# Second-layer modulation parts moved from TensorE to GpSimd, during the first layer's feed-forward

## The chip, the core and the metric

The kernel runs on one core of one Trainium2 chip. The metric is the device time of one execution in microseconds (us). Five engines with queues of their own work side by side: TensorE (PE, with its weight loads as PEld), VectorE (DVE), ScalarE (ACT), GpSimd (POOL) and SyncE (SP). Each takes its instructions in the order in which the build put them. A DMA is issued from the queue of an engine, here SP or POOL, and runs on 16 DMA engines that all share.

## What is computed

A backbone of two layers over 256 latent tokens and 256 context tokens, 1024 channels wide. Each layer forms six modulation vectors from a conditioning vector, and uses them as shift, scale and gate:

```python
mod_l = (silu(c) @ w_mod[i] + b_mod[i])          # latents;  w_mod[i] is 1024 x 6144
mod_c = (silu(c_ctx) @ w_mod[i] + b_mod[i])      # context
sh1, sc1, g1, sh2, sc2, g2 = split(mod, 6)       # each 1024 wide
u   = modulate(rmsnorm(x, norm1_w[i]), sh1, sc1) @ w_in[i]
x   = x + g1 * branch_merge(ssd(u), attention(u), gates(u))
h   = modulate(rmsnorm(x, norm2_w[i]), sh2, sc2)
x   = x + g2 * conv_ffn(h)
```

The last layer (i = 1) gives its result for the latents alone: the context tokens take part only through the first part (sh1, sc1) of its modulation. Its parts g1, sh2, sc2 and g2 are read for latents alone.

## The kernel before

**Tiles and products.** Channels lie on the 128 partitions and tokens along a row, 512 tokens in layer 0 and 256 or 512 in layer 1. Each weight tile is 128 x 1024 numbers (four blocks of 128 rows by 256 columns, 512 KB). It is loaded by SP into `raw`, split by ACT into a rounded part `whi` and by DVE into the rest `wlo` (`split_w`, L313 and L314), and each product takes three matmuls: `whi` with the high part of the activations (`th`), `whi` with the low part (`tl`), `wlo` with `th`. `gemm_f` (L393 to L395 and L407 to L409), `gemm_halves` (L425 to L427, where the two halves s = 0 and s = 1 of 256 tokens are finished one after the other) and `gemm_t` (L441 to L443) do this. They get their tiles from `take`.

**Work in the gaps.** Generators stand in lists. `lanes` hold attention heads, scan steps and norms, and advance by a step every few matmuls. `trickle` holds the modulation parts: `take` advances it by one step for each weight tile. One part g covers 2048 of the 6144 columns of `w_mod[i]`, so a layer has g = 0 (sh1, sc1), g = 1 (g1, sh2) and g = 2 (sc2, g2). `mod_part` works a part off in 16 steps. A step loads 512 KB of `w_mod` on SP's queue into `mraw` (two buffers), and multiplies it with four fp32 matmuls of 32 columns of weights (`s2`, the vectors silu(c) and silu(c_ctx) among zeros) by 256 columns (L465). In the profile one such matmul is two records. At the end the bank goes through ACT and eight records of transposes (L472) to the columns `mod`. Parts (0,1), (0,2) and (1,0) run during layer 0's mixer, parts (1,1) and (1,2) during layer 1's mixer.

**Norms.** `Stats.rstd` sums squares with two matmuls (`pystat`, L516), and DVE makes `ms` of them. POOL raises `ms` to the power of -1/2 (`rs`, L521), DVE writes a diagonal `dg`, and TensorE spreads it (L493). Then for each of the eight blocks of 128 channels `mod_block` runs DVE (`lnv`, L541), ACT twice (`th` L542 and `lnv` L546) and POOL (`tl`, L547). The norm ahead of layer 0's feed-forward is called once for each half, s = 0 and s = 1, from L1098. The norm at the head of layer 1 is queued from L1151 during the last products of the feed-forward. POOL has little else to do: the subtractions of the scan (L969) and its products (L925), and some small DMAs.

**The feed-forward of layer 0.** `w_up` takes 44 weight tiles and `w_down` 30. The last two products of `w_down` have 256 columns each (s = 0 and s = 1), the others 512 after the first two.

**What sets the order.** The order in which instructions stand on each engine is set when the program is built. It follows the code, except that an instruction may be moved ahead of others where the builder holds its inputs to be ready. Buffers of one tag are reused in turn, and the next writer waits for the last reader.

Of the kernel before, what the change touches and what calls it, by code (L numbers as in the profile page):

```python
# [10 lines left out]
F32 = mybir.dt.float32  # L11
F32R = mybir.dt.float32r
AF = mybir.ActivationFunctionType
ALU = mybir.AluOpType
AX = mybir.AxisListType

P = 128
D = 1024
KD = D // P
# [40 lines left out]
def hybrid_backbone_kernel(  # L60
# [7 lines left out]
    V, A, G, T = nc.vector, nc.scalar, nc.gpsimd, nc.tensor  # L68

    base = ctx.enter_context(tc.tile_pool(name="base", bufs=1))  # L70
    wp = ctx.enter_context(tc.tile_pool(name="wp", bufs=1))
    lp = ctx.enter_context(tc.tile_pool(name="lp", bufs=1))
# [3 lines left out]
    def nm(s):  # L76
        cnt[0] += 1
        return f"{s}_{cnt[0]}"

    def bank(tag, what=""):  # L80
        return psp.tile([P, 512], F32, tag=tag, name=nm("p" + tag + what), bufs={"mm": 2, "s": 3, "y": 2, "m": 1}[tag])
# [11 lines left out]
    ident = kt[:, C_ID:C_ID + P]  # L93
# [5 lines left out]
    sinT = kt[:, C_SIN:C_SIN + SEQ]  # L99
    mhalf = base.tile([P, 4], F32, name="mhalf")  # L100
    V.memset(mhalf, -0.5)


    dp = ctx.enter_context(tc.tile_pool(name="dp", bufs=1, space=bass.MemoryType.DRAM))
# [24 lines left out]
    col = []  # L129
# [85 lines left out]
    def boot_load(f):  # L215

        raws = []
        for v in range(2):
            for kq in range(2):
                raw = bp.tile([P, 4, 256], F32, tag="boot", name=nm("boot"), bufs=8)  # L220
                nc.sync.dma_start(raw, kview(w_mod[0], 1024 * (1 - v) + 256 * f, 256, 4 * kq, 4))
                raws.append((raw, v, kq))
        return raws

    def boot_mod(raws):
        ps = bank("s", "mod")
        for raw, v, kq in raws:
            for j in range(4):
                T.matmul(ps[32 * j:32 * j + 32, v * 256:v * 256 + 256], s2[:, 4 * kq + j, :], raw[:, j, :],
                         start=kq == 0 and v == 0, stop=kq == 1 and v == 1)  # L230
        row = lp.tile([P, 512], F32, tag="g", name=nm("modrow"), bufs=4)
        A.copy(row, ps)
        return row
# [19 lines left out]
    with tc.tile_pool(name="rows", bufs=2) as rp:  # L253
# [4 lines left out]
        raws = boot_load(0)  # L258
# [7 lines left out]
        ps = bank("s")  # L266
        T.transpose(ps[:, 0:16], r0, ident[0:16, 0:16])
        s2 = base.tile([P, KD, 32], F32, name="s2")
# [7 lines left out]
        row = boot_mod(raws)  # L276
        load_cols(0, rows0)
        boot_cols(0, row)
        for s in range(2):
# [6 lines left out]
            for j in range(0, KD, 2):  # L286
                ps = bank("s")
# [33 lines left out]
    def fill(n, pinned=False):  # L321
        load(n)
        while loaded and len(ready) < n:
            ready.append(split_w(*loaded.pop(0), pinned))
# [2 lines left out]
    lead = [1]  # L327
    lanes = ([], [])
    trickle = []

    def advance(queue):

        while queue:
            try:
                return next(queue[0]) is not None
            except StopIteration:
                queue.pop(0)
        return False
# [6 lines left out]
    def drip():  # L345
        advance(trickle)
# [9 lines left out]
    def flush():  # L356
        while trickle:
            drip()

    def take(n_tiles):  # L360
        ws = []
        for _ in range(n_tiles):
            fill(1)
            ws.append(ready.pop(0))
            load(DL)
        for _ in range(n_tiles):
            drip()
        fill(lead[0])
        return ws
# [87 lines left out]
    def mod_part(i, g, pool, ps):  # L457

        for half in range(2):
            for k in range(KD):  # L460
                raw = pool.tile([P, 4, 256], F32, tag="mraw", name=nm("mraw"), bufs=2)
                src = w_mod[i, k * P:(k + 1) * P, g * 2048:(g + 1) * 2048]
                nc.sync.dma_start(raw, src.rearrange("p (j h n) -> p h j n", j=4, h=2)[:, half])
                for j in range(4):
                    T.matmul(ps[32 * j:32 * j + 32, half * 256:half * 256 + 256], s2[:, k, :], raw[:, j, :],  # L465
                             start=k == 0, stop=k == KD - 1)
                yield 1
        row = lp.tile([P, 512], F32, tag="g", name=nm("modrow"), bufs=4)
        A.copy(row, ps)
        pt = bank("s")  # L470
        for b in range(4):
            T.transpose(pt[:, b * P:(b + 1) * P], row[:, b * P:(b + 1) * P], ident)  # L472
        m = col[i]["mod"]
        for v in range(2):
            V.tensor_tensor(
                m[:, g * 16:(g + 1) * 16, v].rearrange("p (j b) -> p b j", j=4),
                pt.rearrange("p (b j r) -> p b j r", b=4, j=4)[:, :, :, v],
                col[i]["bm"][:, g * 16:(g + 1) * 16].rearrange("p (j b) -> p b j", j=4), op=ALU.add)
        if g == 0:
            a, sc, nw = col[i]["a1"], m[:, 8:16, :], col[i]["n1"]  # L480
        elif g == 2:
            a, sc, nw = col[i]["a2"], m[:, 32:40, :], col[i]["n2"]
        else:
            return
        V.scalar_tensor_tensor(a, sc, 1.0, nw.unsqueeze(2).to_broadcast([P, KD, 2]), op0=ALU.add, op1=ALU.mult)


    def spread(pool, rs, s, ps):
# [86 lines left out]
    for i in range(DEPTH):  # L575
        if i:
            L = col[i]
            m = L["mod"]
        full = i < DEPTH - 1
# [37 lines left out]
        if i == 0:  # L617
# [3 lines left out]
            L = col[0]  # L621
            m = L["mod"]
            for f in range(4):
                whi, wlo, _ = split_w(*load_w(plan.pop(0)))
                if f < 3:
                    raws = boot_load(f + 1)
# [7 lines left out]
                for cc in range(2):  # L634
                    for fb in range(2):
                        cs = slice(fb * P, fb * P + P)
                        for kk in range(2):
                            k = 2 * f + kk
# [4 lines left out]
                    if cc == 0 and f < 3:  # L643
                        row = boot_mod(raws)
# [2 lines left out]
        xd = park_x(i, N)  # L647
        mst = ExitStack()
        mp = mst.enter_context(tc.tile_pool(name=f"mp{i}", bufs=1))
        mb = bank("m", "mod")  # L650
        trickle.extend(mod_part(*lg, mp, mb) for lg in (((0, 1), (0, 2), (1, 0)) if full else ((1, 1), (1, 2))))
        mg = [mp.tile([P, N], F32, name=f"mg{i}_{j}") for j in range(KD)]
        BF = [mp.tile([P, 512], F32, name=f"BF{i}_{j}") for j in range(4)]
        CF = [mp.tile([P, N], F32, name=f"CF{i}_{j}") for j in range(4)]
# [118 lines left out]
        for z in kLz:  # L773
            for cc in range(2):
                q = slice(64 - 64 * cc, 128 - 64 * cc)
# [38 lines left out]
        ps = bank("mm", "dt")  # L814
        for n, x in enumerate((hh, hl)):
            for k in range(KD):
                T.matmul(ps[32 * (k % 4):32 * (k % 4) + 32, :], wdt[:, k, :], x[k].bitcast(F32),
                         start=n == 0 and k < 4, stop=n == 1 and k > 3)
        if True:
            raw = lp.tile([P, 512], F32, tag="g", name=nm("dtr"), bufs=4)  # L820
            A.copy(raw, ps)
            pt = bank("s")
# [35 lines left out]
            for t in range(4):  # L858
                for dr in range(2):
                    r = 32 * t + 16 * dr  # L860
# [173 lines left out]
        for p in range(4):  # L1034
            for f, o in enumerate(gemm_f(hh, hl, N, KD)):
                j = 2 * p + f
# [26 lines left out]
        for p in range(4):  # L1063
            for f, o in enumerate(gemm_f(yh, yl, N, KD)):
                j = 2 * p + f
# [38 lines left out]
        fp = fst.enter_context(tc.tile_pool(name=f"ff{i}", bufs=1))  # L1104
        fh = [fp.tile([P, N], F32R, name=f"fh{i}_{k}") for k in range(KF)]
        fl = [fp.tile([P, N], F32R, name=f"fl{i}_{k}") for k in range(KF)]
        def ff_conv(ps, n, dst, r):
            conv3(ps, n, dst, lambda k: L["fw"](k, r), L["fb"](r))

# [26 lines left out]
        if full:  # L1136
            st = Stats(lp)
            for p in range(3):
                for f, o in enumerate(gemm_f(fh, fl, N, KF)):
                    for s in range(2):  # L1140
                        residual(2 * p + f, o[:, 256 * s:256 * s + 256], 40, s)
                        st.add(xF[2 * p + f][:, 256 * s:256 * s + 256], s)
            flush()
            hh, hl = operand(lp)
            for s in range(2):
                for f, o in enumerate(gemm_f(fh, fl, 256, KF, 256 * s)):
                    if f == 0:
                        drain()
                    residual(6 + f, o, 40, s)
                    st.add(xF[6 + f][:, 256 * s:256 * s + 256], s)  # L1150
                lanes[0].append(ln_steps(st, lp, i + 1, col[i + 1]["a1"], 0, s, hh, hl))  # L1151
        else:

            st = Stats(lp)
            fwb = fp.tile([P, D], F32, name="fwb")
            G.dma_start(fwb, final_norm_w.partition_broadcast(P))
            ot = [fp.tile([P, D], F32, name=f"ot{t}") for t in range(2)]
            for p in range(4):
                pt = bank("s")
                for f, o in enumerate(gemm_f(fh, fl, N, KF)):  # L1160
                    j = 2 * p + f
                    residual(j, o, 40, 0)
                    st.add(xF[j][:, 0:256], 0)
                    for t in range(2):
                        T.transpose(pt[:, t * 256 + f * P:t * 256 + (f + 1) * P], xF[j][:, t * P:(t + 1) * P], ident)
                for t in range(2):
                    A.copy(ot[t][:, 256 * p:256 * p + 256], pt[:, t * 256:(t + 1) * 256])
            rs, _ = st.rstd(0, D)
            for t in range(2):
                for e in range(2):  # L1170
                    es = slice(512 * e, 512 * e + 512)
                    V.scalar_tensor_tensor(ot[t][:, es], ot[t][:, es], rs[:, t:t + 1], fwb[:, es], op0=ALU.mult, op1=ALU.mult)
                    (nc.sync if e else nc.scalar).dma_start(out[0, t * P:(t + 1) * P, es], ot[t][:, es])
        flush()
        fst.close()


# [29 lines left out]
```

## Time and profile before

| | |
|---|---|
| time, median of 3 runs | 1745.26 us (1743.87 to 1746.32) |
| the profiled execution | 1740.01 us, its span 1738.2 us |
| granted clock of TensorE, mean | 0.993 |
| instructions | 27022 |
| PE busy | 1667.1 us, 96% |
| DVE busy | 1148.0 us, 66% |
| ACT busy | 848.2 us, 49% |
| POOL busy | 181.3 us, 10% |
| DMA | 240.71 MB, 138 GB/s in the mean |

The busy times are sums over stages with different limits. In the profile's rows a line of an engine gives count, busy time and mean duration of a group. In answers by time the columns are start, duration, engine, line, operation, what is written and read, the form, the count, and in brackets the idle time before it with what ended it. Layer 0's mixer takes the time up to about 658 us, its output projection and second norm that up to about 715 us, its feed-forward that up to about 1081 us. Layer 1 follows.

### The profile page before, as it was taken

Reading aid. Unit: us, or ns where it says so; the run is one execution under the profiler, and the core shown is the slowest. Engines: PE = TensorE matmul, PEld = TensorE weight load, DVE = VectorE, ACT = ScalarE, POOL = GpSimd, SP = SyncE. Lnnn points to the kernel's source line nnn. Section 1 sums busy time; section 2 is a strip of 40 time slices with the busy share of each in tenths; the row PEclk is TensorE's granted clock in tenths of the full one; section 3 lists DMA queues with packets and bytes.
Section 4 is the critical chain, followed back from the end, with each engine's and each line's share of the span. In section 5 each row is a group of like instructions: output and inputs, shape, how many; then the busy total and the mean of one; then the engine's idle time right before and its main releaser. Section 6 shows DMA issues by size and latency. Waiting matters only on the chain. (4 is left out here: it accounts for less than half of the span.)

```text
span 1738.2 us, 27022 instructions
## 1 busy us (share of the span) xinstructions
PE 1667.1 (96%) x10547; PEld 1406.2 (81%) x10547; DVE 1148.0 (66%) x2008; ACT 848.2 (49%) x1567; POOL 181.3 (10%) x212
## 2 busy tenths in 40 slices
PE   7999999999988999999999999999999898989997
PEld 4788878777766788888888888788879788989997
DVE  4776667325988855766666326666675789779964
ACT  3565665413545423644444225555655455466653
POOL 3000010001433000300000002100000252010000
PEclk9999999999999999999999999999999999989999
DMA  9644333555443234233323335844535445646653
GB/s 317 215 127 126 115 119 108 166 173 146 121 107 100 74 109 146 74 97 97 97 87 95 92 108 161 255 146 146 152 93 171 121 110 144 199 154 185 193 176 117
DMA packets 233199, 240.71 MB, mean 138 GB/s; under 512 B 10908, under 2 KB 223551, under 8 KB 233071
## 3 DMA queue, kind: packets, MB, share of 16 engines
q1 hardware_dynamic: 230720, 237.14, 45.4%
q8 instruction: 83, 1.36, 0.3%
q0 software_dynamic: 1312, 1.03, 0.2%
q10 hardware_dynamic: 1039, 0.81, 0.1%
q14 instruction: 45, 0.37, 0.1%
HBM read 234.62 MB, written 4.33 MB: 137 GB/s over the span
## 5 line engine op out<-in xcount | busy, mean ns | idle before, releaser
L314 DVE TENSOR_TENSOR wlo<-raw,whi 128x1024 fp32r<-128x1024 f32 (+1 forms) x318 | 388.3, 1221 | 255.7 <-ACT whi L313 254.8
L313 ACT CAST whi<-raw 128x1024 fp32r<-128x1024 f32 (+1 forms) x318 | 329.2, 1036 | 378.4 <-PE pmmmm L408 146.6
L407 PE MATMUL pmmmm<-th,whi 128*128 128x512 f32 x744 | 306.3, 412 | 1.6 <-DVE chv L572 1.6
L408 PE MATMUL pmmmm<-tl,whi 128*128 128x512 f32 x744 | 296.5, 399 | 0.0
L409 PE MATMUL pmmmm<-th,wlo 128*128 128x512 f32 x744 | 295.6, 397 | 0.0
L407 PEld LDWEIGHTS pmmmm<-th,whi 128*128 128x128 f32 x744 | 140.5, 189 | 42.2 <-issue 7.9
L409 PEld LDWEIGHTS pmmmm<-th,wlo 128*128 128x128 f32 x744 | 140.4, 189 | 34.5 <-issue 1.0
L408 PEld LDWEIGHTS pmmmm<-tl,whi 128*128 128x128 f32 x744 | 140.5, 189 | 31.0 <-issue 2.2
L393 PE MATMUL pmmmm<-th,whi 128*128 128x256 f32 x480 | 138.5, 289 | 1.5 <-ACT whi L313 1.3
L395 PE MATMUL pmmmm<-th,wlo 128*128 128x256 f32 x480 | 134.7, 281 | 0.6 <-DVE wlo L314 0.6
L394 PE MATMUL pmmmm<-tl,whi 128*128 128x256 f32 x480 | 134.8, 281 | 0.0
L969 POOL TENSOR_TENSOR cs<-cs,csc 128x512 f32<-128x512 f32 x48 | 69.1, 1454 | 264.0 <-DMA cs<-csd 141.5
L393 PEld LDWEIGHTS pmmmm<-th,whi 128*128 128x128 f32 x480 | 90.7, 189 | 6.2 <-issue 3.8
L394 PEld LDWEIGHTS pmmmm<-tl,whi 128*128 128x128 f32 x480 | 90.8, 189 | 0.7 <-issue 0.4
L395 PEld LDWEIGHTS pmmmm<-th,wlo 128*128 128x128 f32 x480 | 90.6, 189 | 0.8 <-DVE wlo L314 0.8
L409 PE MATMUL psmm<-th,wlo 128*128 128x512 f32 x200 | 79.3, 397 | 0.0
L725 ACT ACTIVATE e<-psscore,nmx 128x512 f32<-128x512 f32 (+1 forms) x96 | 58.1, 610 | 43.5 <-DVE nmx L722 40.5
L408 PE MATMUL psmm<-tl,whi 128*128 128x512 f32 x200 | 79.2, 396 | 0.0
L521 POOL TENSOR_TENSOR rs<-ms,mhalf 128x2 f32<-128x2 f32 x9 | 6.3, 699 | 698.5 <-DVE ms L518 698.5
L407 PE MATMUL psmm<-th,whi 128*128 128x512 f32 x200 | 79.0, 395 | 0.0
L722 DVE TENSOR_REDUCE nmx<-psscore 128x1 f32<-128x512 f32 (+1 forms) x80 | 51.8, 684 | 34.3 <-PE psscore L85 34.2
L441 PE MATMUL pmmmm<-whi,th 128*128 128x256 f32 x256 | 74.3, 290 | 0.0
(346 smaller groups left out, 3899.0 us busy)
## 6 DMA issues: line engine op xcount, KB each, us to landing
raw<-in_w_in_dram SPq DMA_DIRECT2D x124, 512.0 KB, 4.0
raw<-in_w_up_dram SPq DMA_DIRECT2D x88, 512.0 KB, 3.6
mraw<-in_w_mod_dram SPq DMA_DIRECT2D x80, 512.0 KB, 4.7
raw<-in_w_down_dram SPq DMA_DIRECT2D x45, 512.0 KB, 3.6
cs<-csd SPq DMA_DIRECT2D x24, 512.0 KB, 5.8
boot<-in_w_mod_dram SPq DMA_DIRECT2D x16, 512.0 KB, 9.3
raw<-in_w_br_att_dram SPq DMA_DIRECT2D x16, 512.0 KB, 3.6
raw<-in_w_br_ssd_dram SPq DMA_DIRECT2D x16, 512.0 KB, 3.5
```

What stands on the lines that cost most here:

```text
L313: pin(A.copy(hi[:, 0:n, :], raw[:, 0:n, :]))
L314: pin(V.tensor_tensor(lo[:, 0:n, :], raw[:, 0:n, :], hi[:, 0:n, :].bitcast(F32), op=ALU.subtract))
L393: T.matmul(o[f], whi[:, kk, cs], xh, start=first, stop=False)
L394: T.matmul(o[f], whi[:, kk, cs], xl, start=False, stop=False)
L395: T.matmul(o[f], wlo[:, kk, cs], xh, start=False, stop=last)
L407: T.matmul(o, whi[:, k % 4, cs], hi[k][:, 0:n], start=k == 0, stop=False)
L408: T.matmul(o, whi[:, k % 4, cs], lo[k][:, 0:n], start=False, stop=False)
L409: T.matmul(o, wlo[:, k % 4, cs], hi[k][:, 0:n], start=False, stop=k == k_tiles - 1)
L441: T.matmul(b[:, n, :], hi[k][:, ts], whi[:, k % 4, :], start=k == 0 and n == 0, stop=False)
L722: V.tensor_reduce(nmx[:, cc, 0:ng], sc[cc].rearrange("p (g k) -> p g k", g=ng), axis=AX.X, op=ALU.max, negate=True)
L725: A.activation(e[cc][:, g * w:(g + 1) * w], sc[cc][:, g * w:(g + 1) * w], AF.Exp, bias=nmx[:, cc, g:g + 1], accum_out=sm[:, cc, g:g + 1])
L969: G.tensor_tensor(cs[:, dr], cs[:, dr], csc[:, t, 16 * dr + 4 * g:16 * dr + 4 * g + 4].unsqueeze(2).to_broadcast([P, 4, P]), op=ALU.subtract)
```

## The change

Parts (1,1) and (1,2) are no longer multiplied by TensorE in layer 1's mixer. A new generator, `mod_wide`, works on them from layer 0's feed-forward on, for latents alone. It cuts a part into 8 column groups q of 256 columns, and each group into 8 row blocks k. For each of the 64 tiles (q, k) POOL issues a DMA of 128 KB into `mrow` (two buffers), multiplies the tile by the column `s2[:, k, 0:1]`, and adds it to `macc` (two buffers). When the eight tiles of a group are summed, TensorE adds up the 128 partitions of `macc` by two fp32 matmuls with `pick`, a matrix of zeros with one column of ones, so that group q lands in row q of the bank. The order in the generator asks for the sum of group q-1 at step k = 6 of group q, and for the last one after six empty steps. While it runs, `take` advances `trickle` by two steps for each weight tile (`pace`).

```diff
+    pick = base.tile([P, 64], F32, name="pick")
+    V.memset(pick, 0.0)
+    V.memset(pick[:, 32:33], 1.0)
...
+    pace = [1]
...
-        for _ in range(n_tiles):
+        for _ in range(n_tiles * pace[0]):
             drip()
...
+    def mod_wide(i, g, pool, ps):
+
+        tiles = [(q, k) for q in range(8) for k in range(KD)]
+
+        def fetch(q, k):
+            raw = pool.tile([P, 256], F32, tag="mrow", name=nm("mrow"), bufs=2)
+            c0 = g * 2048 + q * 256
+            G.dma_start(raw, w_mod[i, k * P:(k + 1) * P, c0:c0 + 256])
+            return raw
+
+        def total(q, acc):
+
+            for j in range(2):
+                T.matmul(ps[32 * j:32 * j + 32, 0:P], pick[:, 32 - q:64 - q], acc[:, j * P:(j + 1) * P],
+                         start=q == 0, stop=q == 7)
+
+        raws, old = [fetch(*tiles[0])], None
+        for n, (q, k) in enumerate(tiles):
+            if n + 1 < len(tiles):
+                raws.append(fetch(*tiles[n + 1]))
+            yield 1
+            raw, sk = raws.pop(0), s2[:, k, 0:1].to_broadcast([P, 256])
+            if k == 0:
+                acc = pool.tile([P, 256], F32, tag="macc", name=nm("macc"), bufs=2)
+                G.tensor_tensor(acc, raw, sk, op=ALU.mult)
+            else:
+                G.tensor_tensor(raw, raw, sk, op=ALU.mult)
+                G.tensor_tensor(acc, acc, raw, op=ALU.add)
+            if k == 6 and q:
+                total(q - 1, old)
+            if k == KD - 1:
+                old = acc
+        for _ in range(6):
+            yield 1
+        total(7, old)
+        row = lp.tile([P, 512], F32, tag="g", name=nm("modrow"), bufs=4)
+        A.copy(row[0:64, 0:P], ps[0:64, 0:P])
+        pt = bank("s")
+        T.transpose(pt[:, 0:64], row[0:64, 0:P], ident[0:64, 0:64])
...
+        V.tensor_tensor(m[:, g * 16:(g + 1) * 16, 0].rearrange("p (q j) -> p j q", q=8),
+                        pt[:, 0:64].rearrange("p (j r) -> p j r", j=2)[:, :, 0:8],
+                        L["bm"][:, g * 16:(g + 1) * 16].rearrange("p (q j) -> p j q", q=8), op=ALU.add)
...
-        trickle.extend(mod_part(*lg, mp, mb) for lg in (((0, 1), (0, 2), (1, 0)) if full else ((1, 1), (1, 2))))
+        if full:
+            mb = bank("m", "mod")
+            trickle.extend(mod_part(*lg, mp, mb) for lg in ((0, 1), (0, 2), (1, 0)))
...
+        if full:
+            mb = bank("m", "mod")
+            trickle.extend(mod_wide(1, g, fp, mb) for g in (1, 2))
+            pace[0] = 2
...
-            flush()
             hh, hl = operand(lp)
...
         flush()
+        pace[0] = 1
```

Three places of the built order matter to what follows. The first is TensorE's queue in layer 1's mixer, in the second product of C, before the change. L407 to L409 are the three matmuls, `pmmmm` the bank they fill.

```order
L407 MATMUL pmmmm_9705<-th_8898,whi_9683 128x512
L465 MATMUL pmmod_9316<-mraw_9595,s_125 32x256 x4
L408 MATMUL pmmmm_9705<-tl_8899,whi_9683 128x512
L409 MATMUL pmmmm_9705<-th_8898,wlo_9684 128x512
L407 MATMUL pmmmm_9705<-th_8900,whi_9683 128x512
L408 MATMUL pmmmm_9705<-tl_8901,whi_9683 128x512
L465 MATMUL pmmod_9316<-mraw_9631,s_125 32x256 x4
L409 MATMUL pmmmm_9705<-th_8900,wlo_9684 128x512
```

All 32 groups of four `pmmod` matmuls of this stage are gone in the changed kernel, with the transposes behind them and the 32 loads of `mraw` on SP's queue.

The second is POOL's queue at layer 0's second norm. Before the change nothing but the norm's own work stands there (`rs` and `tl`).

```order
L521 TENSOR_TENSOR rs_5536<-ms_5534,mhalf 128x2
L521 TENSOR_TENSOR rs_6341<-ms_6339,mhalf 128x2
L547 TENSOR_TENSOR tl_6252<-lnv_6350,th_6251 128x256
L547 TENSOR_TENSOR tl_6254<-lnv_6355,th_6253 128x256
L547 TENSOR_TENSOR tl_6256<-lnv_6360,th_6255 128x256
```

In the changed kernel the `rs` of half s = 0 (there L573, `rs_6344`) has 18 loads of `mrow` and 31 multiplications and additions ahead of it, and its `tl` (L599) have others between them. The first load waits for the last `tl` of the gated merge on DVE (L1070 before the change), whose memory it takes over. Here is the end of that stretch:

```order
L499 DMA mrow_7048<-in_w_mod_dram 128x256
L518 TENSOR_TENSOR mrow_7048<-mrow_7048,s_128 128x256
L573 TENSOR_TENSOR rs_6344<-ms_6342,mhalf 128x2
L599 TENSOR_TENSOR tl_6255<-lnv_6353,th_6254 128x256
L599 TENSOR_TENSOR tl_6257<-lnv_6358,th_6256 128x256
L516 TENSOR_TENSOR macc_7050<-mrow_6966,s_128 128x256
L599 TENSOR_TENSOR tl_6259<-lnv_6363,th_6258 128x256
L499 DMA mrow_7052<-in_w_mod_dram 128x256
L519 TENSOR_TENSOR macc_7050<-macc_7050,mrow_7048 128x256
L499 DMA mrow_7056<-in_w_mod_dram 128x256
L599 TENSOR_TENSOR tl_6261<-lnv_6368,th_6260 128x256
L599 TENSOR_TENSOR tl_6263<-lnv_6373,th_6262 128x256
```

From `rs_6344` to the last `tl` of half s = 1 there are 19 multiplications and additions and 10 loads of the new work among the two `rs` and sixteen `tl`. The load just ahead of a multiplication of the same buffer (`mrow_7048`) has to land before POOL can go on.

The third is TensorE's queue in the same norm, changed kernel: the first product of the feed-forward for s = 0 (`psmm_6574`), with the sums of the first two groups.

```order
L430 MATMUL psmm_6574<-th_6256,whi_6278 128x256
L505 MATMUL pmmod_6547<-macc_6558,pick 32x128 x2
L505 MATMUL pmmod_6547<-macc_6864,pick 32x128
L431 MATMUL psmm_6574<-tl_6257,whi_6278 128x256
L432 MATMUL psmm_6574<-th_6256,wlo_6279 128x256
```

Before the change the same stretch holds the three matmuls of the product alone. The other fourteen sums stand about four weight tiles apart, up to the last product of `w_down`. There POOL's queue has all of the new work ahead of the `rs` of layer 1's first norm.

More of the change, by code (lines that the diff above doesn't have):

```diff
@@ L485, in mod_part @@
         V.scalar_tensor_tensor(a, sc, 1.0, nw.unsqueeze(2).to_broadcast([P, KD, 2]), op0=ALU.add, op1=ALU.mult)
+    def mod_wide(i, g, pool, ps):
[32 more added lines that the diff above has]
+        T.transpose(pt[:, 0:64], row[0:64, 0:P], ident[0:64, 0:64])
+        L = col[i]
+        m = L["mod"]
+        V.tensor_tensor(m[:, g * 16:(g + 1) * 16, 0].rearrange("p (q j) -> p j q", q=8),
+                        pt[:, 0:64].rearrange("p (j r) -> p j r", j=2)[:, :, 0:8],
+                        L["bm"][:, g * 16:(g + 1) * 16].rearrange("p (q j) -> p j q", q=8), op=ALU.add)
+        if g == 2:
+            V.scalar_tensor_tensor(L["a2"][:, :, 0], m[:, 32:40, 0], 1.0, L["n2"], op0=ALU.add, op1=ALU.mult)
     def spread(pool, rs, s, ps):
@@ L649, in hybrid_backbone_kernel @@
         mp = mst.enter_context(tc.tile_pool(name=f"mp{i}", bufs=1))
-        mb = bank("m", "mod")
-        trickle.extend(mod_part(*lg, mp, mb) for lg in (((0, 1), (0, 2), (1, 0)) if full else ((1, 1), (1, 2))))
+        if full:
+            mb = bank("m", "mod")
+            trickle.extend(mod_part(*lg, mp, mb) for lg in ((0, 1), (0, 2), (1, 0)))
         mg = [mp.tile([P, N], F32, name=f"mg{i}_{j}") for j in range(KD)]
```

## The prediction

> **What bounds the kernel now.** I read the page's busy times first, then the table by stretches, then the chain of waits and the time line where the change cuts in.
>
> ```profile
> PE 1667.1 (96%) x10547; PEld 1406.2 (81%) x10547; DVE 1148.0 (66%) x2008; ACT 848.2 (49%) x1567; POOL 181.3 (10%) x212
> POOL 3000010001433000300000002100000252010000
> 0.00:100.00 100.00, 84.78 (x531) 60.30 (x532) 60.62 (x165) 44.73 (x85) 14.19 (x30) 1.00 0.80 257
> 659.00:689.00 30.00, 30.00 (x131) 24.09 (x130) 13.47 (x23) 8.81 (x16) 0.00 (x0) 1.00 0.49 158
> 800.00:900.00 100.00, 100.00 (x430) 80.38 (x429) 65.78 (x81) 42.35 (x54) 0.00 (x0) 1.00 0.31 94
> 1100.00:1300.00 200.00, 197.35 (x1405) 162.06 (x1404) 131.95 (x276) 113.04 (x235) 8.12 (x14) 1.00 0.51 154
> ```
>
> The last four rows are stretches: length, then busy time of PE, PEld, DVE, ACT and POOL, the granted clock, and the DMA engines' share. TensorE is the bound in layer 0's feed-forward (800 to 900, no idle time) and nearly so in layer 1's mixer (1100 to 1300, 197.35 of 200). What leaves its queue there is time won. POOL is empty from 659 to 689 and from 800 to 900. That looks like free room, but a queue in order is free only if nothing urgent stands behind the new work.
>
> **Removed in layer 1's mixer.** First the records of the old multiplications and PE's waits in this stage, then the chain at one such place and the transposes.
>
> ```profile
> 1096.70:1302.00 205.30, 19.80 (x256) 5.80 (x256) 0.58 (x1) 1.00 0.52 156
> PE pmmod L465 <- DMA mraw<-in_w_mod_dram: 2.5, 5, 0.8
> 1099.24 5.54 DMA mraw<-in_w_mod_dram
> 1104.82 0.64 PE pmmod L465 x8
> 1105.46 0.43 PE pmmmm L408
> 1107.28 0.24 PE pmmmm L409
> 1174.62 0.44 PE ps L472 x4
> ```
>
> The 256 records take 19.80 us of PE. A matmul behind a group takes 0.43 where the next of its kind takes 0.24, so each turn costs 0.19; the 32 steps stand singly or in pairs, 16 to 32 turns, and with 24 that is 4.6. PE waited 2.5 for `mraw`. Two sets of eight transposes, one of them with four records at 0.44, make with their turns about 2 x 0.63 = 1.3 (in one set part of the records lies elsewhere). Together 28. The 2.5 may turn into a wait for weights on the same SP queue, so I take 26, between 23 and 28. SP's queue also loses 32 loads of 512 KB, which can only help there.
>
> **Added on TensorE.** 16 sums of two fp32 matmuls, four records of 128 columns each, and two short transposes. The trace has no such matmul; the nearest row is `pystat`, four records of 128 columns.
>
> ```profile
> 696.78 0.71 PE L516 MATMUL pystat<-kt,acc 128*128 128x128 f32 x4
> 699.04 0.70 PE L493 MATMUL pystat<-dg,kt 128*128 128x256 f32 x2 [0.61 <-DVE dg L491]
> 697.83 0.70 POOL L521 TENSOR_TENSOR rs<-ms,mhalf 128x2 f32<-128x2 f32 x1 [104.89 <-DVE ms L518]
> ```
>
> Its 0.71 includes a modelled tail that overlaps the next matmul, so 0.71 is a ceiling; the floor is half the old group of 0.64, 0.32. I take 0.5: 16 x 0.5 = 8, plus 0.6 for the transposes, 8.6 in all (5.5 to 12). PE alone therefore gains 26 - 8.6 = 17.4.
>
> **POOL's price for one tile.** Rows on the operations and on loads from POOL's queue:
>
> ```profile
> L925 POOL TENSOR_TENSOR xd<-xT,ddt x48: 606/616/1524, 428.6 to 1461.8; 128x256 f32<-128x256 f32 x48
> L925 POOL TENSOR_TENSOR xd<-xT,ddt 128x256 f32<-128x256 f32 x48 | 36.3, 764 | 51.4 <-PE psstate L85 33.8 <-DVE xT L910 17.6
> L203 POOL DMA_DIRECT2D lb<-in_diff_lambda_dram x1 | 0.6, 570 | 37.8 <-PE pmmod L465 37.8
> csd<-csr POOLq DMA_DIRECT2D x16, 8.0 KB, 1.6
> lb<-in_diff_lambda_dram POOLq DMA_DIRECT2D x1, 128.0 KB, 5.4
> fwb<-in_final_norm_w_dram POOLq DMA_DIRECT2D x1, 512.0 KB, 6.1
> ```
>
> The first row gives minimum, median and maximum in ns: an operation of the same size takes 0.61 undisturbed, 0.76 in the mean where DVE is busy. Issuing a load costs POOL 0.57. No row shows a 128 KB load in a calm stage. `csd` landed after 1.6 with little to move, `lb` with the same 128 KB after 5.4 at a DMA share of 0.80, `fwb` after 6.1 with four times as much. Here the share is 0.49 and then 0.31, so I take the midpoint of 1.6 and 5.4, 3.5. With two `mrow` buffers, load n+2 starts when tile n is added; two tiles take a landing, a multiplication and an addition: (3.5 + 2 x 0.61 + 0.1) / 2 = 2.4 a tile, and 2.6 with 0.76.
>
> [...]
>
> **The second norm of layer 0: the largest cost.** Its rows on DVE and POOL, half s = 0 and half s = 1:
>
> ```profile
> 658.02 0.68 DVE L1070 SCALAR_TENSOR_TENSOR tl<-mg,th 128x512 fp32r<-128x512 f32 x1
> 701.43 0.74 POOL L547 TENSOR_TENSOR tl<-lnv,th 128x256 fp32r<-128x256 f32 x1 [2.90 <-ACT lnv L546]
> 706.41 2.32 POOL L547 TENSOR_TENSOR tl<-lnv,th 128x256 fp32r<-128x256 f32 x3 [0.16 <-ACT lnv L546]
> 710.55 0.70 POOL L521 TENSOR_TENSOR rs<-ms,mhalf 128x2 f32<-128x2 f32 x1 [1.83 <-DVE ms L518]
> 714.40 1.42 POOL L547 TENSOR_TENSOR tl<-lnv,th 128x256 fp32r<-128x256 f32 x2 [3.15 <-ACT lnv L546]
> 719.20 1.69 POOL L547 TENSOR_TENSOR tl<-lnv,th 128x256 fp32r<-128x256 f32 x2 [0.17 <-ACT lnv L546]
> ```
>
> POOL may start its tiles when DVE's last `tl` of the merge ends, at 658.7, and has 17 tiles ahead of `rs`, the last waiting for its own load in full: 658.7 + 3.5 + 0.7 + 15 x 2.41 + 0.55 + 3.5 + 0.6 = 703.7. Today `rs` starts at 697.83, and PE already stands at the spreading matmul for 0.61 then, so nothing covers the difference: 6 us lost (0 with a landing of 2.6, 24 with 5.4).
>
> Then come the new operations among the `tl`: 19 of 0.61 to 0.76 and 10 issues of 0.57, 17 to 20 us. POOL's idle time between the last `tl` of s = 0 and the first of s = 1 (1.83 + 3.15) takes 5 of them, and about four landings, not yet there when their multiplication comes up, give back 4: 16 more until the last `tl`, which ends at 720.9 today. PE cannot fill this time, for in its order the products of s = 1 and their spread come before the rest of s = 0. Its remaining work behind the last `tl` is the same as before, so the delay carries over: 6 + 16 = 22 us.
>
> **The rest of the feed-forward.** At 430 matmuls in 100 us a weight tile (24) takes PE 5.6, a step of `trickle` 2.8. POOL's 2.6 keeps pace, and two `macc` buffers hold it from running ahead. At the end the weight tiles have 256 columns and PE is twice as fast, while the last group can start only when the sixth sum has freed its buffer: 8 x 2.6 less the 1.3 won by two loads already landed, 19.5, against some 165 matmuls of 0.115, 19. With `rs` behind, 2 us of stall (0 to 14 at a landing of 4.5).
>
> ```profile
> 1065.51 0.70 POOL L521 TENSOR_TENSOR rs<-ms,mhalf 128x2 f32<-128x2 f32 x1 [344.63 <-DVE ms L518]
> 1359.14 2.09 DVE L975 TENSOR_TENSOR cc<-cc,CF 128x1024 f32<-128x1024 f32 x1
> 1361.15 2.06 DVE L314 TENSOR_TENSOR wlo<-raw,whi 128x1024 fp32r<-128x1024 f32 x1
> 1359.11 3.02 POOL L969 TENSOR_TENSOR cs<-cs,csc 128x512 f32<-128x512 f32 x2 [1.27 <-ACT cc L966]
> L314 DVE TENSOR_TENSOR wlo<-raw,whi x318: 691/1225/2055, 23.8 to 1722.1; 128x1024 fp32r<-128x1024 f32 x159
> ```
>
> The first row is the `rs` of layer 1's norm, after 344 idle us; behind POOL's backlog it stands last. The others show that DVE and POOL hold each other up when both read two operands of SBUF: `wlo` took 2.06 beside POOL's subtractions, 1.225 in the median. That can cost the feed-forward's weight tiles up to 0.84 each. PE needs 5.6 for a tile, which hides it; I put 1 us for the few that don't hide (0 to 6). The two memsets of `pick` lie at the start, where DVE waits for loads: nothing.
>
> **Sum.** -26 + 8.6 + 22 + 2 + 1 = +7.6. On the profiled execution, 1740.0, that is 1747.6; the median of the runs shown is 5.3 above the profiled one, so 1745.3 + 7.6 = 1753.
>
> **Rivals.**
>
> Short landing. If a load lands in about 2.5, POOL is through at 696 and `rs` isn't late. The interleaving still costs 16: -26 + 8.6 + 16 + 0 + 1, about zero, 1745, decided at a landing of 2.8. For it speaks `csd` with 1.6, against it `lb` with 5.4. [...]
>
> POOL can't keep pace. Above a landing of 4.2 a tile takes 2.9 and more with disturbed operations, PE's 2.8 outruns POOL, and PE waits at the sums. At 4.5: 32 for the norm, 14 at the end, +30; at 5.4, 46 + 60, about +90. `lb` speaks for it, the low DMA share against it. Middle 1785.
>
> More was won in layer 1. The chain shows five long transits of `mraw`, of which the row above is the longest, 5.54; at some 5 each that is 25 us. If the chain is right and PE's 2.5 wrong, the gain is 48 and the sum -14: 1731. Against it stands the row of waits, and PE's 197.35 busy of 200; it decides only if the gain exceeds 34.
>
> DVE starves TensorE. If 30 of the 74 feed-forward tiles come 0.5 late: +15 on the sum, 1768. [...]
>
> **Chances.** Forecast 0.57, short landing 0.18, POOL behind 0.13, more won 0.07, DVE starving 0.05. No change is within 0.2% (3.5 us), about what can be told apart. Of the forecast's case 0.07 lies within it; of the short landing 0.05 lies below, 0.11 within, 0.02 above. Faster 0.07 + 0.05 = 0.12, same 0.18, slower 0.70. The range leaves out most of "more won" below and the upper part of "POOL behind": 1741 to 1785.
>
> **What would show it.** No `pmmod` records after 1096; `rs` of the norm starting near 704 instead of 697.8, with PE waiting at the spread; the last `tl` of s = 1 some 22 later than 720.9; `mrow` loads landing near 3.5. The prediction is wrong if these loads land under 2.8 or over 4.2, or if PE's gain in layer 1 is far from 17.

## The result, and the profile after the change

| | median of the runs | runs | profiled span | granted clock |
|---|---|---|---|---|
| before | 1744.97 us | 1743.87 to 1746.32 | 1738.2 us | 0.993 |
| changed | 1767.89 us | 1764.42 to 1769.26 | 1762.6 us | 0.982 |

The changed kernel is slower: 1.0127 times the time before, 95% interval 1.0111 to 1.0143, 22.9 us. The forecast of 1753 had the sign and a third of the size; 1767.9 lies inside the range.

Two lines of the page answer to those shown of before: the busy times, then GpSimd and the granted clock in 40 slices of 44 us.

```profile
PE 1664.6 (94%) x10349; PEld 1409.6 (80%) x10349; DVE 1173.1 (67%) x2008; ACT 848.2 (48%) x1567; POOL 452.0 (26%) x580
POOL 3000010001343007723775667500010252010000
PEclk9999999999999999799999999899999999989999
```

GpSimd is busy 271 us longer, in the stretch that was empty. PE issues 198 records fewer and yet is busy only 2.5 us less: look at the clock, where slices 17 and 26 now show 7 and 8. Those two slices hold the second norm of layer 0 and the first norm of layer 1.

The table by stretches puts the loss in its places. Each row is a stretch, its length, the busy time of PE, PEld, DVE, ACT and POOL, the granted clock, the DMA engines' share and GB/s. The ends are set to the same work in both kernels. First the kernel before: second norm of layer 0, the middle of the feed-forward, its end, the first norm of layer 1, layer 1's mixer.

```profile
658.00:721.70 63.70, 61.27 (x369) 53.31 (x368) 34.72 (x67) 29.73 (x61) 13.22 (x18) 1.00 0.34 108
721.70:959.00 237.30, 237.30 (x1052) 192.25 (x1052) 160.03 (x206) 102.29 (x136) 0.00 (x0) 1.00 0.32 97
959.00:1065.50 106.50, 106.37 (x536) 89.14 (x535) 36.12 (x51) 28.08 (x39) 0.00 (x0) 1.00 0.37 113
1065.50:1100.00 34.50, 30.75 (x253) 28.53 (x252) 26.83 (x45) 25.90 (x52) 17.16 (x22) 1.00 0.63 183
1100.00:1477.70 377.70, 365.01 (x2655) 313.66 (x2654) 268.36 (x499) 204.75 (x400) 53.88 (x56) 1.00 0.50 146
```

The same five of the changed kernel:

```profile
659.00:749.50 90.50, 69.03 (x372) 59.34 (x372) 41.03 (x66) 30.57 (x61) 67.40 (x98) 0.88 0.39 122
749.50:991.00 241.50, 241.50 (x1080) 192.90 (x1080) 173.32 (x205) 101.66 (x135) 132.68 (x173) 1.00 0.41 125
991.00:1112.60 121.60, 111.28 (x567) 90.90 (x565) 43.83 (x52) 29.72 (x40) 83.76 (x118) 0.97 0.48 146
1112.60:1150.00 37.40, 34.22 (x253) 32.21 (x254) 27.43 (x47) 26.35 (x53) 16.75 (x23) 0.91 0.47 125
1150.00:1501.70 351.70, 341.37 (x2390) 304.78 (x2390) 265.99 (x494) 202.26 (x397) 53.85 (x56) 1.00 0.41 113
```

Subtract row from row, and within a row the busy time from the length, which gives PE's idle time:

| stretch | length | PE idle | PE busy |
|---|---|---|---|
| second norm of layer 0 | +26.8 | +19.0 | +7.8 |
| feed-forward, middle | +4.2 | 0 | +4.2 |
| feed-forward, end | +15.1 | +10.2 | +4.9 |
| first norm of layer 1 | +2.9 | -0.6 | +3.5 |
| mixer of layer 1 | -26.0 | -2.4 | -23.6 |
| sum | +23.0 | +26.2 | -3.2 |

The mixer gave its 26. Two stalls took 42 back, and the middle of the feed-forward 4. The column of busy times shows a second thing: outside the mixer PE is busy 20.4 us longer, and the 16 sums are not all of it. What one sum costs is seen where it stands among 512-column matmuls of the feed-forward (start, duration, engine, line, operation):

```profile
836.84 0.39 PE L414 MATMUL pmmmm<-th,wlo 128*128 128x512 f32 x1
837.16 0.41 PE L505 MATMUL pmmod<-macc,pick 128*32 128x128 f32 x4
837.50 0.50 PE L412 MATMUL psmm<-th,whi 128*128 128x512 f32 x1
837.84 0.39 PE L413 MATMUL psmm<-tl,whi 128*128 128x512 f32 x1
```

From the first row's start to the last's there are 1.00 us, in which two ordinary matmuls would take 2 x 0.233 (their spacing just before, 836.61 to 836.84). A sum is 0.53, sixteen are 8.5, with the transposes about 9. Of the other 11 of the 20.4 most lies in the norms, where the clock column reads 0.88, 0.97 and 0.91 for 1.00. The rows of PE there show how, the idle time before an instruction and its releaser in brackets:

```profile
709.69 1.22 PE L545 MATMUL pystat<-dg,kt 128*128 128x256 f32 x2 [10.36 <-DVE dg L543]
...
711.13 0.41 PE L430 MATMUL pmmmm<-th,whi 128*128 128x256 f32 x1
...
713.57 0.28 PE L430 MATMUL pmmmm<-th,whi 128*128 128x256 f32 x1
...
732.17 1.22 PE L545 MATMUL pystat<-dg,kt 128*128 128x256 f32 x2 [4.03 <-DVE dg L543]
```

After PE has stood for 10.36 us, a matmul of 256 columns takes 0.41 and not 0.28, and starts come 0.21 apart instead of 0.12, until 713.4. The wait for the next half, 4.03, brings the same. So each of the two waits costs its idle time and then some microseconds at half speed (until 713.4 and 737.3).

What PE waits for is `dg`, which needs `rs`, which needs GpSimd. GpSimd's rows ahead of the first `rs`, and ahead of the `rs` of layer 1:

```profile
703.14 0.58 POOL L499 DMA_DIRECT2D mrow<-in_w_mod_dram  x1 [0.30 <-POOL macc L519]
703.73 0.62 POOL L518 TENSOR_TENSOR mrow<-mrow,s 128x256 f32<-128x256 f32 x1
704.44 0.72 POOL L519 TENSOR_TENSOR macc<-macc,mrow 128x256 f32<-128x256 f32 x1
705.45 0.58 POOL L499 DMA_DIRECT2D mrow<-in_w_mod_dram  x1 [0.30 <-POOL macc L519]
707.88 0.61 POOL L518 TENSOR_TENSOR mrow<-mrow,s 128x256 f32<-128x256 f32 x1 [1.85 <-DMA mrow<-in_w_mod_dram]
708.46 0.72 POOL L573 TENSOR_TENSOR rs<-ms,mhalf 128x2 f32<-128x2 f32 x1
...
1064.83 0.58 POOL L499 DMA_DIRECT2D mrow<-in_w_mod_dram  x1 [0.30 <-POOL macc L519]
1068.62 0.60 POOL L518 TENSOR_TENSOR mrow<-mrow,s 128x256 f32<-128x256 f32 x1 [3.22 <-DMA mrow<-in_w_mod_dram]
1069.20 0.60 POOL L516 TENSOR_TENSOR macc<-mrow,s 128x256 f32<-128x256 f32 x1
...
1111.91 0.72 POOL L519 TENSOR_TENSOR macc<-macc,mrow 128x256 f32<-128x256 f32 x1
1112.60 0.72 POOL L573 TENSOR_TENSOR rs<-ms,mhalf 128x2 f32<-128x2 f32 x1
```

A calm tile is 2.31 us (703.14 to 705.45), and GpSimd is hardly idle in it but for the 0.30 between an addition and the next issue: issue 0.58, multiplication 0.62, addition 0.72 and the gaps are the tile, not the landing. At the start of a group, where the multiplication of its second tile stands ahead of the one that begins the accumulator (L518, then L516), a landing of 1.9 to 3.8 shows. `rs` stands directly behind the last tile in both places.

### The profile page after: what moved, and what is told of

Read it like the earlier page. It is cut to its first block, busy times and chain, and to the rows that moved or that the text cites. A ratio compares the mean times of both kernels' runs of the same rounds, so it can differ in the third digit from the quotient of the medians.

```text
span 1762.6 us, 26949 instructions
## 1 busy us (share of the span) xinstructions
PE 1664.6 (94%) x10349; PEld 1409.6 (80%) x10349; DVE 1173.1 (67%) x2008; ACT 848.2 (48%) x1567; POOL 452.0 (26%) x580
## 4 chain that ended last, share of the span: by engine, by line
PE 63%; issue 9%; POOL 8%; DVE 8%; DMA 6%; ACT 5%; ACTq 0%; SPq 0%; POOLq 0%; DVEq 0%
PE pmmmm L412 8%; PE pmmmm L414 8%; PE pmmmm L413 8%; PE pmmmm L398 3%; PE pmmmm L400 3%; PE pmmmm L399 3%; PE psmm L412 3%; PE psmm L413 3%; PE psmm L414 3%; PE psmm L399 3%; PE psmm L398 3%; PE psmm L400 2%; DMA mrow<-in_w_mod_dram 2%; POOL macc L519 2%; DMA cs<-csd 2%
## 5 line engine op out<-in xcount | busy, mean ns | idle before, releaser
L318 DVE TENSOR_TENSOR wlo<-raw,whi 128x1024 fp32r<-128x1024 f32 (+1 forms) x318 | 399.7, 1257 | 242.3 <-ACT whi L317 241.4
L809 POOL TENSOR_TENSOR rsa<-ss,mhalf 128x4 f32<-128x4 f32 (+1 forms) x16 | 13.7, 857 | 380.5 <-DVE ss L807 380.5
L519 POOL TENSOR_TENSOR macc<-macc,mrow 128x256 f32<-128x256 f32 x112 | 105.1, 939 | 7.7
L499 POOL DMA_DIRECT2D mrow<-in_w_mod_dram x128 | 73.9, 577 | 105.6 <-issue 69.7
L518 POOL TENSOR_TENSOR mrow<-mrow,s 128x256 f32<-128x256 f32 x112 | 79.0, 705 | 49.7 <-DMA mrow<-in_w_mod_dram 48.1
```

The costliest lines, as they stand in the source:

```text
L318: pin(V.tensor_tensor(lo[:, 0:n, :], raw[:, 0:n, :], hi[:, 0:n, :].bitcast(F32), op=ALU.subtract))
L499: G.dma_start(raw, w_mod[i, k * P:(k + 1) * P, c0:c0 + 256])
L518: G.tensor_tensor(raw, raw, sk, op=ALU.mult)
L519: G.tensor_tensor(acc, acc, raw, op=ALU.add)
```

## The experiments

Three explanations were set against each other. Q: GpSimd's queue is in order, its new tiles stand ahead of the `rs` of two norms, and PE's wait there is made longer by the clock. P: the work itself costs, because VectorE and GpSimd hold each other up or because of the sums on PE, wherever it stands. T: an idle PE costs its idle time alone. Changes are shown against the changed kernel unless the text says otherwise; ratios are to the kernel before on the same chip.

**The removal alone.**

```
-            mb = bank("m", "mod")
-            trickle.extend(mod_wide(1, g, fp, mb) for g in (1, 2))
-            pace[0] = 2
+            mm_ = col[1]["mod"]
+            V.tensor_copy(mm_[:, 16:48, 0], col[1]["bm"][:, 16:48])
...
```

> Only the removal: the two late modulation groups of layer 1 are neither formed in layer 1's mixer nor on GpSimd; their bias alone is copied, so the products are left out. This prices what leaving layer 1's mixer is worth by itself. Theory Q (GpSimd's queue in order: new tiles stand ahead of the work of both norms, and PE's idle time there also lowers the granted clock): the mixer is 26 us shorter and nothing else moves, about 1719. Rival M (the gain itself was smaller or larger than 26): under 1712 or over 1726.

Measured 1721.9, ratio 0.9873 (0.9851 to 0.9895), 22 us faster. From the `rs` of layer 1's second half to the end of its mixer the kernel before took 393.2 us, this one 371.0: 22.2 less. The changed kernel takes 367.7 for it, 25.5 less. The gain was there, and the 3 between the two are TensorE's clock, not the stall ahead. In this stretch this run has 10.2 us at half clock, the changed kernel and the kernel before 3.4. All seven traces without the products in layer 1 part in the same way: the three with 10.2 take 369.8 to 371.0 us, the four with 3.4 take 367.5 to 367.9.

**The start behind the norm.**

```
-        raws, old = [fetch(*tiles[0])], None
+        with tc.issue_after(last[0].ins):
+            raws, old = [fetch(*tiles[0])], None
...
-            G.tensor_tensor(l[:, ss], v, h[:, ss].bitcast(F32), op=ALU.subtract)
+            last[0] = G.tensor_tensor(l[:, ss], v, h[:, ss].bitcast(F32), op=ALU.subtract)
```

> The changed kernel with one difference: GpSimd's new loads and operations may only start behind the last subtraction of layer 0's second norm. Theory Q: the first rs of that norm starts near 698 again, PE's waits at the spread fall from 16 to under 2 us there, the granted clock stays at 1.00 there, and 27 us come back; the start is 60 us later, but GpSimd had waited 63 us for its ring of two accumulators, so the end of the feed-forward should be no more than some 10 later: 1741 to 1755. Rival P (the loss is VectorE and GpSimd holding each other up on their SBUF side, or the 16 sums on PE): the same work is done, so the time stays within 5 of 1768.

Measured 1752.4, ratio 1.0050 (1.0032 to 1.0068). The stretch of the norm, and PE's two largest waits in the feed-forward and the norms:

```profile
663.50:727.00 63.50, 61.06 (x372) 53.30 (x371) 34.34 (x65) 30.50 (x62) 14.38 (x20) 1.00 0.33 110
...
PE pystat L548 <- DVE dg L546: 12.5, 4, 11.1
PE pmmod L506 <- POOL macc L522: 10.4, 5, 4.1
```

The norm is as long as before, 63.5 against 63.7, at a clock of 1.00: all of the 26.8 is undone by moving the start, with the same loads, operations and sums. Explanation P, which gave 1763 to 1773, falls. Only 13 (by the ratios) to 15.5 us (by the medians) of it reach the time. GpSimd starts 63 us later and takes 376 us for its 128 tiles, 2.94 each: PE now waits at the sums (10.4, of which 4.1 at the first one, with 6.8 us of half clock behind it), and the wait at layer 1's norm is still 11.1. GpSimd's time for a tile is the second half of the matter.

**The sums earlier.**

```
-            if k == 6 and q:
+            if k == 2 and q:
```

> The changed kernel with one difference: a group's sum on PE is issued at the third instead of the seventh step of the next group, so an accumulator comes free four steps (about 11 us) earlier. Theory Q: the last group can start some 10 us earlier, rs of layer 1's first norm starts some 10 us sooner, PE's wait of 10.4 there goes and with it the half clock behind it, 12 to 15 us in all: 1753 to 1757; the second norm of layer 0 keeps its loss. Rival R (GpSimd is simply too slow for the 256-column end, whatever the ring does): under 4 us come back, 1764 to 1768.

In the changed kernel GpSimd's accumulators waited 63.4 us in four places for a sum to free one of the two:

```profile
  PE pmmod L505: 63.4, 4
```

Measured 1756.2, ratio 1.0073 (1.0049 to 1.0098). Layer 1's `rs` starts at 1102.6 and not 1112.6, and PE's waits for `dg` fall from 25.9 us in the four norm halves to 14.7:

```profile
1102.62 0.71 POOL L573 TENSOR_TENSOR rs<-ms,mhalf 128x2 f32<-128x2 f32 x1 [0.46 <-DVE ms L570]
...
PE pystat L545 <- DVE dg L543: 14.7, 4, 9.5
```

As explanation Q had it: the end of the feed-forward was late because its groups were let start late (the thirteenth of the sixteen now begins at 1010.1 and not at 1019.1), and 9 (by the ratios) to 12 us (by the medians) come back from one number. The 9.5 that is left as the longest wait is that of layer 0's norm. R, a GpSimd too slow whatever the ring, falls for this place. The norm of layer 0 keeps its loss (`rs` at 708.5).

**The subtractions on VectorE.**

```
-            mod_block(pool, i, a, sh0, j, s, bc, hi[j], lo[j])
+            mod_block(pool, i, a, sh0, j, s, bc, hi[j], lo[j], eng)
...
-                ln_half(st, lp, i, L["a2"], 24, s, hh, hl)
+                ln_half(st, lp, i, L["a2"], 24, s, hh, hl, V)
```

> The changed kernel with one difference: the 16 subtractions of layer 0's second norm are done on VectorE, not on GpSimd; rs stays on GpSimd. It parts the loss at that norm in two. Theory Q: rs of the first half is as late as before (708, 10 us of it), since it still stands behind 17 tiles; what the tiles between the subtractions cost goes, some 10 of the 27 us, so 1756 to 1760. If the late rs were all of it, 1768; if the subtractions were all of it, 1741 to 1745.

Measured 1762.3, ratio 1.0109 (1.0081 to 1.0137): 3 (by the ratios) to 5.6 us (by the medians) came back where 8 to 12 were expected. The first `rs` is as late as in the changed kernel, and so is the second, at 731.5 against 730.5, although no subtraction stands before it any more:

```profile
708.76 0.71 POOL L573 TENSOR_TENSOR rs<-ms,mhalf 128x2 f32<-128x2 f32 x1
731.47 0.73 POOL L573 TENSOR_TENSOR rs<-ms,mhalf 128x2 f32<-128x2 f32 x1
PE pystat L545 <- DVE dg L543: 29.2, 4, 14.3
```

In this norm PE waited 14.4 us for the two `rs` and 6.8 for the subtractions in the changed kernel; here it waits 14.3 for the two `rs`, and 1.9 for a `wlo` of VectorE, which took over some of the subtractions' price. So the two `rs` behind tiles are the larger part. Within the norm 5.7 us came back (the matmul that starts at 749.8 in the changed kernel starts at 744.1), and some 3 of them went again at layer 1's norm, where PE waited 14.3 and not 10.9.

**Pauses in the kernel before.** GpSimd gets small dependent operations of 0.69 us ahead of `rs`, in the first half of layer 0's second norm and of layer 1's first norm; nothing else differs from the kernel before.

```
+            if hold[0]:
+                G.tensor_tensor(slow, slow, ms[:, 0:1].to_broadcast([P, 256]), op=ALU.mult)
+                for _ in range(hold[0] - 1):
+                    z = G.tensor_tensor(slow, slow, ms[:, 0:1].to_broadcast([P, 256]), op=ALU.mult)
+                with tc.issue_after(z.ins):
+                    G.tensor_tensor(rs, ms, mhalf[:, 0:2], op=ALU.pow)
+                hold[0] = 0
+                return rs, ps
...
+                st.hold = 13
...
+                st.hold = 4
```

> The kernel before with nothing but two pauses: 13 small dependent operations on GpSimd (about 8 us) ahead of rs of the first half of layer 0's second norm, and 4 (about 2.5 us) ahead of rs of the first half of layer 1's first norm. It prices an idle PE by itself. Theory Q with the clock: the long pause costs its own length and, since the granted clock falls to a half for some 3.5 us behind it, about 1.8 more; the short one perhaps half of that: 12 to 14 us in all over the kernel before. Rival T (an idle PE costs its idle time alone): 10 to 11, with PE's busy time unchanged.

> The same two places with 6 and 2 operations (about 3.7 and 1.2 us). Theory Q with the clock: the pause of 3.7 still brings the half clock (in the changed kernel waits of 4.03 and 1.62 did), that of 1.2 does not (1.12 did not): 6 to 7 us in all. Rival T: 5, and no stretch of half clock behind either.

Measured 1760.0, ratio 1.0078 (1.0061 to 1.0096), 14 us; and 1755.3, ratio 1.0052 (1.0033 to 1.0070), 9 us. PE's rows at the two places, of the longer pauses and then of the shorter:

```profile
713.51 1.22 PE L496 MATMUL pystat<-dg,kt 128*128 128x256 f32 x2 [6.72 <-DVE dg L494]
...
1086.56 0.70 PE L496 MATMUL pystat<-dg,kt 128*128 128x256 f32 x2 [2.21 <-DVE dg L494]
1088.03 0.42 PE L397 MATMUL pmmmm<-fl,whi 128*128 128x256 f32 x1
```

```profile
703.98 0.70 PE L496 MATMUL pystat<-dg,kt 128*128 128x256 f32 x2 [2.83 <-DVE dg L494]
704.80 0.42 PE L428 MATMUL pmmmm<-th,whi 128*128 128x256 f32 x1
...
714.55 0.41 PE L430 MATMUL psmm<-th,wlo 128*128 128x256 f32 x1
...
1076.83 0.70 PE L496 MATMUL pystat<-dg,kt 128*128 128x256 f32 x2 [1.38 <-DVE dg L494]
```

Waits of 6.72, 2.83 and 2.21 are followed by matmuls of 0.41 to 0.42, that of 1.38 is not. Behind the 2.21 the matmuls first run in 0.28 and go to 0.42 at 1087.8. The next rows are two windows of 3.41 us, one up to there and one from there on, with the columns of the table by stretches. PE was busy for 1.23 us of the first, and in the second the clock is 0.50:

```profile
1084.38:1087.79 3.41, 1.23 (x8) 1.18 (x9) 1.71 (x3) 0.00 (x0) 1.59 (x3) 1.00 0.00 0
1087.79:1091.21 3.42, 3.42 (x18) 3.42 (x17) 3.42 (x6) 2.68 (x6) 0.35 (x1) 0.50 0.29 84
```

The best price is that of the wait of 2.83. It made `rs` 4.0 late (702.77 against 697.83 before, less the 1.0 by which that run was behind already at the `rs` of the norm before it, 591.9 against 590.9). From there to the next half's `rs` the run took 16.0 us where the kernel before takes 12.7: 3.3 more, at half clock from 704.7 to 715.0: four fifths of the pause on top of it. Explanation T, 5 us for the shorter pauses, falls: 9.1 with an interval from 5.8 to 12.2. For the longer ones its 10 to 11 lies at the lower edge of the interval (10.6 to 16.8), and the rows decide. From the `rs` of the norm before (at 590.9 in the kernel before) to layer 1's first `rs`, the run with the shorter pauses takes 9.1 longer than the kernel before and that with the longer ones 14.2, while the pauses themselves, by GpSimd's rows, are 5.3 and 11.5.

**A third accumulator.** The start behind the norm is kept.

```
-                T.matmul(ps[32 * j:32 * j + 32, 0:P], pick[:, 32 - q:64 - q], acc[:, j * P:(j + 1) * P],
-                         start=q == 0, stop=q == 7)
+                T.matmul(ps[:, 2 * q + j:2 * q + j + 1], acc[:, j * P:(j + 1) * P], ones[:, 0:1], start=True, stop=True)
...
-                acc = pool.tile([P, 256], F32, tag="macc", name=nm("macc"), bufs=2)
+                acc = pool.tile([P, 256], F32, tag="macc", name=nm("macc"), bufs=3)
```

> The start behind the norm as before in these runs, and a third accumulator; to make room for it each sum over the partitions is one matmul with a single moving column of ones that lands its result as a column, so the 64-column table, the copy and the transposes go too. Theory Q: a multiplication no longer stands in line before the accumulator's, so no load's landing is laid bare at a group's start; GpSimd's tile falls from 2.97 to about 2.65 us, its last tile ends near 1070 instead of 1104, PE doesn't wait at the sums, and the time is 1728 to 1738. If GpSimd is held up by VectorE rather than by its own queue, the tile stays near 2.9 and the time at 1748 or more.

Measured 1751.4, ratio 1.0026 (1.0007 to 1.0044): a miss. GpSimd's groups of this stretch (busy, mean ns of one, then idle time before them and its releasers):

```profile
L518 POOL TENSOR_TENSOR macc<-macc,mrow 128x256 f32<-128x256 f32 x112 | 98.8, 882 | 8.2
L517 POOL TENSOR_TENSOR mrow<-mrow,s 128x256 f32<-128x256 f32 x112 | 88.5, 790 | 43.4 <-DMA mrow<-in_w_mod_dram 41.8
L497 POOL DMA_DIRECT2D mrow<-in_w_mod_dram x128 | 75.0, 586 | 40.0 <-POOL macc L518 32.3 <-POOL macc L515 4.5 <-issue 3.2
...
PE pystat L538 <- DVE dg L536: 11.1, 4, 9.7
```

The tile is 2.86 us (366 in 128), hardly less than 2.94. These rows say where it goes: 1.55 for the operations (98.8, 88.5 and 11.7 for the groups' first tiles), 0.59 for the issue and 0.31 around it, 0.34 for landings that still show. In the trace the first six groups begin with their own multiplication, but in the other ten that of the second tile still stands ahead of it (L517, then L515), and 1.9 to 2.5 us of a landing show at each. The third accumulator removed the waits on the ring and not this order; the reading behind the expectation was wrong, and the rival's number was nearer. PE still waited 4.0 at the first sum and 9.7 at layer 1's norm. Against the calm 0.62 and 0.72 of above, the means of 0.79 and 0.88 add 0.3 a tile. That goes with VectorE: all 24 operations of over 1.2 us lay beside a `wlo`, though so did 44 of the 176 of under 0.8.

**The loads on SyncE's queue**, three load buffers, two accumulators, the sum at the fifth step, otherwise as the run before.

```
-            G.dma_start(raw, w_mod[i, k * P:(k + 1) * P, c0:c0 + 256])
+            tc.keep_in_program_order(nc.sync.dma_start(raw, w_mod[i, k * P:(k + 1) * P, c0:c0 + 256]))
...
```

> As the run beside it, but with two accumulators, three load buffers, the sum at the fifth step, and the 128 loads issued on SyncE's queue between the weight loads. Theory Q: GpSimd no longer spends 0.58 on the issue and 0.30 around it, a tile takes 1.4 to 2.0, it always leads PE, no wait is left at either norm, and the time is that of the kernel without the products (1722) plus 16 sums and little else: 1724 to 1733. Rival S: the loads, waiting in SyncE's queue for their buffers, hold back the weights behind them, and PE waits for wlo: 1745 and more.

Measured 1727.0, ratio 0.9886 (0.9867 to 0.9906): about 20 us faster than the kernel before, and by the medians 41 faster than the changed one. GpSimd is busy 396 us, the issues gone; PE's waits for `dg` are those of before, and `rs` of layer 1 finds GpSimd idle for 7 us:

```profile
PE pystat L539 <- DVE dg L537: 2.0, 4, 0.6
...
1076.61 0.71 POOL L567 TENSOR_TENSOR rs<-ms,mhalf 128x2 f32<-128x2 f32 x1 [7.04 <-DVE ms L564]
...
714.90:1076.60 361.70, 360.69 (x1722) 297.71 (x1723) 230.36 (x272) 139.31 (x195) 220.39 (x249) 1.00 0.45 144
```

From one `rs` to the next this stretch is 361.7 us; without the products (the first experiment) it is 355.1. The whole price of the new work, beside a GpSimd that keeps ahead, is 6.6 us. Fifteen of the sixteen sums, here of one column, lie in it. One of them takes 0.45 (from the matmul ahead of it, at 881.82, to the third behind it, at 882.97, are 1.15, and three matmuls alone take 3 x 0.233), fifteen 6.7: that is all of it, and next to nothing is left that VectorE and GpSimd, holding each other up, could cost PE. VectorE is as busy as in the changed kernel (1173.6 against 1173.1), so whatever its `wlo` lose to GpSimd stays mostly hidden. The queue, the load buffers, the accumulators and the step of the sum were changed together, and what each gives was not measured apart; the issue and the gap around it, 0.90 a tile in the run before, are gone from GpSimd's rows.

## Why the prediction missed

**Layer 1's mixer, 26 forecast, 25.5 to 26.0 measured.** The count of records, turns and waits held. The rival "more was won" is out.

**The sums, 8.6 forecast, about 9 measured** (0.53 each against 0.5 taken).

**VectorE and GpSimd holding each other up, 1 forecast.** In the middle of the feed-forward the stretch grew by 4.2, and seven sums and a transpose are 4.0. The rival in which VectorE starves TensorE is out: `wlo` in the mean went from 1.22 us to 1.26 over the span and from 1.23 to 1.37 in this stretch, where PE waited for none.

**The second norm of layer 0, 22 forecast, 26.8 measured.** The place, the queue and the wait at the spread were right. The idle time was even slightly overrated (19.0). What failed is a term that was not in the sum: "PE cannot fill this time" was priced at the idle time alone, and the half clock behind the waits added about 6.7 (7.8 more busy, less two sums). The inner split was off as well: the first `rs` was 10 late and not 6, the second cost another 4.0 for which nothing was put, and the interleaving with the subtractions, priced at 16, made PE wait 6.8 and gave back 5.7 when it was taken away. That 22 came so near is in part luck.

**The end of the feed-forward, 2 forecast, 15 measured, and 2.9 more in the norm behind it, where the clock was 0.91.** This is the term that was most wrongly sized. The step was "8 x 2.6 less the 1.3 won by two loads already landed, 19.5, against some 165 matmuls". GpSimd's last full groups took 25.5 and 24.0 us (their first operations start at 1043.7, 1069.2 and 1093.2), 3.0 to 3.2 a tile. Nor did the last group wait for a sum: the one that freed its buffer was done at 1081.7, and GpSimd came to it at 1093.2. The formula for the tile, a landing and two operations over two buffers, left out what GpSimd itself spends: 0.58 for the issue and 0.30 ahead of it. It came out near the calm truth, 2.4 against 2.31, because the landing put in was too long:

```profile
mrow<-in_w_mod_dram POOLq DMA_DIRECT2D x128, 128.0 KB, 2.5
L519 POOL TENSOR_TENSOR macc<-macc,mrow 128x256 f32<-128x256 f32 x112 | 105.1, 939 | 7.7
```

The landing was 2.5 in the median, where 3.5 had been put in. The rival "short landing" had its condition met, 2.5 under 2.8, and still its time of 1745 did not come: the tile did not depend on the landing as its formula said. The last row is the other half: an addition takes 0.94 in the mean where 0.61 to 0.76 was put in. The estimate came from another operation, GpSimd's product in the scan (L925).

**The rival "POOL can't keep pace"** named the mechanism at the end, but tied it to a landing above 4.2. Its condition belonged on the tile's own time.

**The sum by what the runs show**: -26.0 for the mixer, +26.8 and +15.1 for the two stalls, +2.9 at layer 1's norm, +4.2 in the middle, 23.0; a further 1.4 of the profiled 24.4 lies ahead of the norm and at the end, where the code is the same.

## What to carry to other kernels

An engine that looks empty in the profile still has a queue in order: list the urgent instructions that come behind the new work on it (here two `rs` of 0.7 us), and start the work behind the one and end it before the other. Price a unit of background work by everything its engine issues for it, the load's issue and the gap around it too (here 0.58 and 0.30 of a tile's 2.31 us), and let another queue issue the loads if that engine is the slow one. When a stall is put on TensorE, count its idle time and then the half clock behind it (here 3.7 us of it behind a wait of 10.36, none behind one of 1.38).

## What the runs showed of the hardware

- TensorE's granted clock fell to 0.50 in or right behind waits of 10.36, 6.72, 4.03, 2.83, 2.21 and 2.06 us, and not at 1.38 or 1.12. The length of one wait didn't decide it: in the changed kernel a wait of 1.62 with smaller ones around it was enough (at 720.3), and one of 2.55 was not (at 1387.6).
- In the traces of the kernel before and of the changed one, between 200 and 1600 us, half clock came in 13 stretches: eight of 3.41 us, one of 6.83, three of 10.24 and one of 13.65. In the 3.41 us ahead of the half clock PE was busy for 1.23 with the wait of 2.21, and for 1.56 with that of 1.62. With the wait of 2.55 it was busy for 1.58 of 3.42 us (1385.8 to 1389.2), and the clock stayed at 1.00. So how much idle time brings the half clock is not shown.
- After the wait of 10.36 half clock lasted another 3.7 us (709.7 to 713.4), where work followed without a break. With the wait of 2.83, and waits of 0.8 and 1.4 behind it, it lasted 10.2 in all (704.7 to 715.0).
- Between the end of a GpSimd addition and the issue of a load that waits for its buffer lie 0.30 us, at each of the 107 places that the changed kernel's trace puts down to it, 32 us in all.
- A load of 128 KB landed in 2.5 us in the median when GpSimd issued it and in 3.3 when SyncE did. The run with SyncE's was the faster all the same; in it the issue takes none of GpSimd's time.
